# A constant tile 32 bytes longer: all tiles of matrix operands begin at a multiple of 128 bytes in each partition

## The chip, the cores and the metric

The kernel runs on one core of a Trainium2 chip. The metric is the device time of one execution in microseconds (us). Each partition of the on-chip memory (128 partitions) holds 224 KiB, and this kernel fills it almost to the last byte.

## What is computed

One layer with two parallel branches over a sequence of 256 rows of width 2048, all in float32:

```
h = rms_norm(x, norm_g);  proj = h @ w_in            # 2048 -> 11264 columns
q, k, v, z_a, u_b, v_b, z_b, g_a, g_b = split(proj)
att  = softmax(causal(rms_norm(q) rms_norm(k)^T / sqrt(128))) v     # 8 heads of 128
y_a  = (att * silu(z_a)) @ w_proj_a
sgu  = gelu(u_b) * (causal(w_spatial) @ rms_norm(gelu(v_b)) + b_spatial)
y_b  = (sgu * silu(z_b)) @ w_proj_b
out  = x + (sigmoid(g_a) * y_a + sigmoid(g_b) * y_b) @ w_out
```

## The kernel before, in words

**The stream of weights.** All weights pass through the core once, as 120 steps of 1 MB (128 partitions x 2048 words). `schedule` lists them in order: eight steps ("quad") each for q, k, v, za, vb, ub and zb, then four times eight steps of the gates g followed by four steps "proj" of the two branch projections, then sixteen steps of the output projection. SyncE's queue loads a step into one of six buffers `words`; ScalarE rounds it into a float32r tile `wh` (the high half), and VectorE writes the rest, the low half, back into the same buffer `words`, seen as float32r. `split` and `halve` (L228 to L266) do this, two or three steps ahead of the matmuls (the table `LEADS`).

**The matmuls.** Every product is made of three matmuls, recorded at one line, L416, in the helper `three`: low half of the activations with high half of the weights, high with high, high with low. The weights are the moving operand (512 columns), the activations the stationary operand (128 x 128). So of three matmuls in a row the first two stream a tile `wh` and the third streams `words`. 66 of the 120 steps are multiplied directly (24 matmuls; 16 of these are the "proj" steps), and 54 steps by a scheme with seven products in place of eight (21 matmuls); for the latter VectorE forms three sums of blocks into a buffer `sums` (L260 to L262), ScalarE rounds them into a tile `th` (L263), and VectorE takes the remainders in `words` (L265) and in `sums` (L266). That makes 2,718 matmuls of 512 columns. Between them stand transposes (L528, L588), the scores (L550), the attention's second product (L600, L602) and the spatial mixing (L616), all of 128 columns.

**The order on the engines** is written out by hand: `HOOKS` says behind which step each piece of the attention, the gating and the norms is issued, and all engines keep that order (`manual_schedule`).

**Where the tiles lie.** The six buffers `words` and three buffers `sums` are cut out of one block, `arena`, that starts in each partition at byte 1152, nine times 128, and all their sizes are multiples of 128. Behind it come the pools, in the order in which they are opened (L168 to L172): `const`, `big` (ten slots of 8192 bytes: the halves of the activations `xuh`, `xul`, `mh`, `ml`, `zah` and so on, the forms `Fhx`, `Flx`, the transposed `qT`, `kT`), `unit` (ten slots of 2048 bytes), `wpool` (four `wh` of 8192, three `th` of 6144) and `small`. A tile begins at the next multiple of 32 bytes. In `const` the order and the offsets are:

| tile | bytes | offset from a multiple of 128, before | after |
|---|---|---|---|
| vec | 104 | 0 | 0 |
| ident | 512 | 0 | 0 |
| mhalf | 32, then 64 | 0 | 0 |
| tri | 512 | 32 | 64 |
| gain | 512 | 32 | 64 |
| rstd | 8 | 32 | 64 |
| ssum | 8 | 64 | 96 |
| F5h, F5l | 2048 each | 96 | 0 |
| all of big, unit, wpool | 8192, 2048, 6144 | 96 | 0 |
| words and sums (arena) | 8192, 6144 | 0 | 0 |

So before, every stationary operand and the moving tiles `wh` and `th` begin 96 bytes past a multiple of 128, and the moving low halves (`words`, `sums`) at one. Slices of them that a matmul reads begin at multiples of 512 bytes from the start of the tile, so each matmul's operand has its tile's offset. The last tile of `small` ends 32 bytes below the end of the partition.

Of the kernel before, what the change touches and what calls it, by code (L numbers as in the profile page):

```python
# [14 lines left out]
F32 = mybir.dt.float32  # L15
# [7 lines left out]
P = 128  # L23
# [106 lines left out]
def hybrid_layer_kernel(  # L130
# [37 lines left out]
    const = ctx.enter_context(tc.tile_pool(name="const", bufs=1))  # L168
# [3 lines left out]
    small = ctx.enter_context(tc.tile_pool(name="small", bufs=4))  # L172
# [152 lines left out]

    ident = const.tile([P, P], F32, name="ident")
    make_identity(nc, ident)
    mhalf = const.tile([P, 8], F32, name="mhalf")
    nc.gpsimd.memset(mhalf[:, 0:4], -0.5)
    ninf = mhalf[:, 4:5]  # L330
    nc.gpsimd.memset(ninf, NEG_INF)
# [226 lines left out]
    def scores(hg, c):  # L558
        return X["S0", hg] if c == 0 else X["S1"][:, 4 * hg:4 * hg + 4, :]

    def soft_max(hg):
        for c in range(2):
            mx = small.tile([P, 4], F32, tag="mx", name="mx")
            nc.vector.reduce_max(mx, scores(hg, c), axis=AX.X)
            nm = X["nm", c, hg] = small.tile([P, 4], F32, tag="nm", name="nm")
            nc.vector.tensor_scalar_mul(nm, mx, -ATT_SCALE)
# [160 lines left out]
    def keep_vec():  # L727
        nc.scalar.copy(vec, vec0)

    fns = dict(load_nat=load_nat, keep_vec=keep_vec, forms_4=forms_4, forms_5=forms_5, forms=forms, stats=stats,  # L730
               halves_h=halves_h, halves_l=halves_l, halves_4=halves_4, squares=squares, root=root, norm=norm,
               turn_qk=turn_qk, score=score, soft_max=soft_max, soft_exp=soft_exp, soft_sum=soft_sum, turn_p=turn_p,
               func=func, attend=attend, load_mix=load_mix, turn_z=turn_z, causal_mix=causal_mix, mix=mix,
               spatial=spatial, gate_b=gate_b, turn_m=turn_m, forms_m4=forms_m4, halves_m4=halves_m4,
# [176 lines left out]
```

## Time and profile before

| | us |
|---|---|
| median of 3 runs | 670.65 (670.46 to 672.16) |
| the profiled execution | 671.46 |
| its span, from the first to the last instruction | 669.7 |
| PE (matmuls) busy | 663.1 (99%) |
| PEld (loads of the stationary operand, beside PE) busy | 539.4 (81%) |
| DVE (VectorE) busy | 598.0 (89%) |
| ACT (ScalarE) busy | 425.8 (64%) |
| POOL (GpSimd) busy | 59.1 (9%) |

Outside the span lie 1.8 us of the profiled execution. A matmul's recorded time runs from its start to the modelled end of its results, and the next one starts before that; the pace is read from start to start. In the rows below, "out<-moving,stationary" names a matmul's operands.

### The profile page before, as it was taken

The numbers are of one execution on the slowest core, as the hardware profiler recorded it, in microseconds if no ns is written. First come the engines' busy times: TensorE is split into PE (matmuls) and PEld (weight loads), VectorE is DVE, ScalarE is ACT, GpSimd is POOL, SyncE is SP. The second block draws the span as 40 slices with busy tenths as digits, with TensorE's granted clock in tenths as the row PEclk, the third lists the DMA queues.
The fourth block names the chain that finished last, engine by engine and source line by source line (L and its number), as shares of the span: only waits on it lengthen the run. The fifth ranks groups of instructions, "written<-read, shape, count | busy, mean of one in ns | idle before, by whom it ended". The sixth has DMA issues, their size and how long they took to land.

```text
span 669.7 us, 8157 instructions
## 1 busy us (share of the span) xinstructions
PE 663.1 (99%) x2974; PEld 539.4 (81%) x2974; DVE 598.0 (89%) x577; ACT 425.8 (64%) x534; POOL 59.1 (9%) x72
## 2 busy tenths in 40 slices
PE   8999999999999999999999999999999999999997
PEld 5888888888888888888888888888888888887885
DVE  4879998898978899899999899899989997899995
ACT  7968759957958567796465555654564556365450
POOL 1000203100000101200010001000100000000000
PEclk9999999999999999999999999999999999999999
DMA  8985686885677766786788579858975895786831
GB/s 299 419 319 186 242 237 224 266 238 187 220 227 208 258 201 223 260 224 248 211 292 253 188 243 276 293 188 260 294 235 197 273 291 182 246 259 222 247 126 63
DMA packets 42519, 159.46 MB, mean 238 GB/s; under 512 B 4720, under 2 KB 5360, under 8 KB 33264
## 3 DMA queue, kind: packets, MB, share of 16 engines
q1 hardware_dynamic: 34704, 144.80, 60.2%
q0 software_dynamic: 6624, 12.06, 12.3%
q10 hardware_dynamic: 1152, 2.10, 1.1%
q8 instruction: 23, 0.38, 0.2%
q14 instruction: 16, 0.13, 0.1%
HBM read 156.84 MB, written 26.21 MB: 273 GB/s over the span
## 4 chain that ended last, share of the span: by engine, by line
PE 98%; DMA 1%; ACT 0%; DVE 0%; SPq 0%; DVEq 0%; issue 0%
PE acc_g L416 15%; PE y L416 13%; PE acc_out L416 9%; PE seven_g L416 9%; PE acc_q L416 7%; PE acc_k L416 5%; PE acc_v L416 5%; PE acc_vb L416 5%; PE acc_zb L416 5%; PE acc_za L416 5%; PE acc_ub L416 5%; PE seven_out L416 3%; PE seven_k L416 2%; PE seven_zb L416 2%; PE seven_vb L416 2%; PE seven_za L416 2%
## 5 line engine op out<-in xcount | busy, mean ns | idle before, releaser
L214 POOL DMA_DIRECT2D ring<-in_w x46 | 38.3, 846 | 400.4 <-DMA ring<-in_w 400.4
L263 ACT CAST th<-sums1float 128x1536 fp32r<-128x1536 f32 x18 | 26.8, 1487 | 51.3 <-DVE sums1float L262 51.3
L263 ACT CAST th<-sums0float 128x1536 fp32r<-128x1536 f32 x18 | 26.6, 1479 | 44.1 <-DVE sums0float L262 44.1
L263 ACT CAST th<-sums2float 128x1536 fp32r<-128x1536 f32 x18 | 26.6, 1480 | 34.3 <-DVE sums2float L262 29.1
L416 PE MATMUL acc_g<-wh,xuh 128*128 128x512 f32 x105 | 41.3, 393 | 0.0
L416 PE MATMUL acc_g<-wh,xul 128*128 128x512 f32 x105 | 40.9, 390 | 0.0
L230 DVE TENSOR_TENSOR words5float32r<-words5float,wh 128x2048 fp32r<-128x2048 f32 x14 | 32.0, 2286 | 3.6 <-ACT wh L229 3.6
L266 DVE TENSOR_TENSOR sums1float32r<-sums1float,th 128x1536 fp32r<-128x1536 f32 x18 | 31.5, 1753 | 3.2 <-ACT th L263 3.2
L230 DVE TENSOR_TENSOR words4float32r<-words4float,wh 128x2048 fp32r<-128x2048 f32 x13 | 29.7, 2287 | 4.4 <-ACT wh L229 4.4
L266 DVE TENSOR_TENSOR sums2float32r<-sums2float,th 128x1536 fp32r<-128x1536 f32 x18 | 31.5, 1752 | 0.2 <-ACT th L263 0.2
L266 DVE TENSOR_TENSOR sums0float32r<-sums0float,th 128x1536 fp32r<-128x1536 f32 x18 | 31.6, 1753 | 0.0
L265 DVE TENSOR_TENSOR words2float32r<-words2float,wh 128x2048 fp32r<-128x2048 f32 x12 | 27.5, 2292 | 1.2
L416 PE MATMUL acc_out<-wh,mh 128*128 128x512 f32 x72 | 28.4, 394 | 0.0
L416 PE MATMUL acc_out<-wh,ml 128*128 128x512 f32 x72 | 28.3, 393 | 0.0
L416 PE MATMUL acc_q<-wh,xuh 128*128 128x512 f32 x64 | 26.3, 411 | 1.1 <-ACT wh L229 1.1
L229 ACT CAST wh<-words5float 128x2048 fp32r<-128x2048 f32 x14 | 26.6, 1904 | 0.1
L416 PE MATMUL acc_q<-wh,xul 128*128 128x512 f32 x64 | 25.9, 404 | 0.0
L229 ACT CAST wh<-words4float 128x2048 fp32r<-128x2048 f32 x13 | 24.9, 1916 | 1.5 <-PE y L416 0.9
L230 DVE TENSOR_TENSOR words1float32r<-words1float,wh 128x2048 fp32r<-128x2048 f32 x9 | 20.6, 2287 | 5.5 <-ACT wh L229 5.5
L416 PE MATMUL y<-wh,zal 128*128 128x512 f32 x64 | 25.2, 393 | 0.0
L416 PE MATMUL y<-wh,zah 128*128 128x512 f32 x64 | 25.2, 393 | 0.0
L416 PE MATMUL y<-wh,zbh 128*128 128x512 f32 x64 | 25.2, 393 | 0.0
(960 smaller groups left out, 2151.2 us busy)
## 6 DMA issues: line engine op xcount, KB each, us to landing
words4float<-in_w SPq DMA_DIRECT2D x15, 1024.0 KB, 6.5
words5float<-in_w SPq DMA_DIRECT2D x14, 1024.0 KB, 4.9
ring<-in_w SPq DMA_DIRECT2D x46, 256.0 KB, 6.6
ring<-in_w POOLq DMA_DIRECT2D x46, 256.0 KB, 6.9
words0float<-in_w SPq DMA_DIRECT2D x11, 1024.0 KB, 6.9
words1float<-in_w SPq DMA_DIRECT2D x11, 1024.0 KB, 8.3
words3float<-in_w SPq DMA_DIRECT2D x11, 1024.0 KB, 8.2
words2float<-in_w SPq DMA_DIRECT2D x11, 768.0 KB, 6.7
```

Source lines behind the costliest of these rows:

```text
L214: nc.gpsimd.dma_start(pre[i], w[i, :, B:2 * B], accum_op=ALU.add)
L229: nc.scalar.copy(h, r)
L230: nc.vector.tensor_tensor(l, r, f(h), op=ALU.subtract)
L263: nc.scalar.copy(th[i], t)
L265: nc.vector.tensor_tensor(wl[i], r, f(wh[i]), op=ALU.subtract)
L266: nc.vector.tensor_tensor(tl[i], t, f(th[i]), op=ALU.subtract)
L416: nc.tensor.matmul(acc, a, b, start=(start and n == 0), stop=(stop and n == 2))
```

## The change

The constant tile `mhalf` gets 16 words in place of 8, so 64 bytes in place of 32. Only words 0 to 4 of it are used, before and after. What is allocated behind it moves up by 32 bytes. To make room, the tile `mx` of the softmax (16 bytes, each in a place of 32) gets two buffers in place of the four that the pool gives by default, which frees 64 bytes at the end of the partition.

```diff
-    mhalf = const.tile([P, 8], F32, name="mhalf")
+    mhalf = const.tile([P, 16], F32, name="mhalf")
     nc.gpsimd.memset(mhalf[:, 0:4], -0.5)
     ninf = mhalf[:, 4:5]
...
-            mx = small.tile([P, 4], F32, tag="mx", name="mx")
+            mx = small.tile([P, 4], F32, tag="mx", bufs=2, name="mx")
             nc.vector.reduce_max(mx, scores(hg, c), axis=AX.X)
             nm = X["nm", c, hg] = small.tile([P, 4], F32, tag="nm", name="nm")
             nc.vector.tensor_scalar_mul(nm, mx, -ATT_SCALE)
```

## The prediction

> **What bounds the kernel now.** I read the profile's page first: who is busy, at which clock, and what the chain that ended last is made of.
>
> ```profile
> span 669.7 us, 8157 instructions
> ...
> PE 663.1 (99%) x2974; PEld 539.4 (81%) x2974; DVE 598.0 (89%) x577; ACT 425.8 (64%) x534; POOL 59.1 (9%) x72
> ...
> PEclk9999999999999999999999999999999999999999
> ...
> PE 98%; DMA 1%; ACT 0%; DVE 0%; SPq 0%; DVEq 0%; issue 0%
> ```
>
> TensorE is the chain: 98% of it, at the full granted clock. Since a busy PE is not PE at its peak, I asked next whether it ever waits (the waits of PE: microseconds in total, times, longest).
>
> ```profile
> PE ps_w L314 <- DVE warm L311: 1.3, 1, 1.3
> PE acc_q L416 <- ACT wh L229: 1.1, 1, 1.1
> ```
>
> That is all before a matmul; so the time is the number of matmuls times the interval from one start to the next. The chain in order of time gives that interval (start, us, line, count).
>
> ```profile
> 52.97 12.60 PE acc_k L416 x54
> ...
> 151.30 5.36 PE ps_s L550 x48
> ...
> 325.57 12.51 PE acc_g L416 x54
> ...
> 431.43 22.19 PE y L416 x96
> ```
>
> The reader is to divide. 12.60/54 is 233.3 ns, 12.51/54 is 231.7, 22.19/96 is 231.1. It is the same instruction each time (128x512, three per product), the same clock, no wait, and yet three paces. They are steady: I followed the intervals between starts through the whole timeline, and each stretch keeps its pace until a transpose or another 128-column instruction breaks the row; then it takes one of the three. Sorted so, 385 intervals run at 233.3 (up to 102 us), 1,149 at about 231.7 and 1,143 at 231.1 ns: 2,677 in all. The other 41 of the 2,718 matmuls stand in the slow start or beside a break.
>
> A pace that depends on how a row was entered, and then stays, is a rhythm that repeats. It repeats over three matmuls: 3 x 233.33 is 700.0 ns and 3 x 231.11 is 693.3; the middle one closes only after twelve, 12 x 231.67 = 2,780. All three are whole multiples of one step of 6.67 ns: 105, 104 and 417 of them. So something in the operand reads seems to be granted in turns of 6.67 ns, and what decides the turn differs between the three matmuls of a product. The groups by line, in the window of the fast rhythm and in that of the slow one, show which:
>
> ```profile
> L416 PE MATMUL y<-wh,zbh 128*128 128x512 f32 x16 | 6.3, 393 | 0.0
> L416 PE MATMUL y<-wh,zbl 128*128 128x512 f32 x16 | 6.2, 388 | 0.0
> ...
> L416 PE MATMUL y<-words0float32r,zbh 128*128 128x512 f32 x8 | 3.2, 398 | 0.0
> ```
>
> ```profile
> L416 PE MATMUL acc_q<-wh,xuh 128*128 128x512 f32 x24 | 9.5, 395 | 0.0
> L416 PE MATMUL acc_q<-wh,xul 128*128 128x512 f32 x24 | 9.4, 393 | 0.0
> L416 PE MATMUL acc_q<-words5float32r,xuh 128*128 128x512 f32 x8 | 3.2, 400 | 0.0
> ```
>
> A recorded time is the interval plus a tail that stays: the mean of 388, 393 and 398 is 393, less 231.1 leaves 162 ns. So in the fast rhythm the three take 226, 231 and 236 ns. The long one is each time the third, which streams `words`. It differs from the other two in its place in the order and in one more thing: `words` begins at a multiple of 128 bytes, `wh` and the stationary tiles 96 bytes past one. The shortest interval, 226 to 227 ns, is 34 steps of 6.67.
>
> **The change part by part.** *Offsets.* After the change `wh`, `th`, `words`, `sums` and all stationary tiles have the same offset, none. No instruction is added or removed; what changes is the interval. If the offset is what tells the three matmuls apart, they become alike, the rhythm closes after one matmul instead of three, and the interval itself must be a whole number of steps: 34 (226.67 ns) or 35 (233.33). The mean is now 34.7. I take 34, because two reads at one offset follow each other in 226 ns in the fast rhythm, and because what makes the third long there, the move from one offset to the other and back, is gone. Term by term: 385 x (233.33 - 226.67) = 2.6 us, 1,149 x (231.67 - 226.67) = 5.7 us, 1,143 x (231.11 - 226.67) = 5.1 us; together 13.4 us. The bounds of this term: 35 steps everywhere cost 1,149 x 1.67 + 1,143 x 2.22 = 4.5 us; one step below 34 (220 ns), for operands that no longer begin inside a turn, would save 2,677 x 11.67 = 31.2 us. Nothing in the trace is as short as 220.
>
> The Trainium skill (TensorE: Matmul & The Clock Gate, "Back-to-back issue gap") gives N/2.4 + 2.5 ns between isolated matmuls, 216 ns for 512 columns. By that figure, as an estimate, some 42 us would be there to be won; the trace's 231 does not agree with it, and no run here shows which part of the difference is the offset's.
>
> *Loads of the stationary operand.* They lie under the matmul before:
>
> ```profile
> L416 PEld LDWEIGHTS acc_g<-wh,xul 128*128 128x128 f32 x105 | 19.7, 188 | 4.6
> ```
>
> 188 ns against an interval of 227 leaves cover, so a shorter load saves nothing by itself.
>
> *Instructions of 128 columns.* The scores, whose operands lie at 96, take 5.36/48 = 111.7 ns each. Some 250 records are of that size; even two or three ns off each is under 0.8 us, in either direction, and I count it at nothing.
>
> *What a faster TensorE runs into.* VectorE prepares the weights:
>
> ```profile
> 300.00:400.00 100.00, 100.00 (x442) 81.34 (x441) 94.44 (x89) 59.76 (x45) 6.58 (x8) 1.00 0.75 235
> 400.00:500.00 100.00, 100.00 (x434) 81.11 (x434) 92.69 (x80) 55.41 (x40) 8.23 (x10) 1.00 0.83 261
> 500.00:600.00 100.00, 100.00 (x451) 81.61 (x450) 90.40 (x89) 54.90 (x48) 6.57 (x8) 1.00 0.76 241
> ```
>
> VectorE is busy 90 to 94 us of each 100 in the gates; TensorE would need 98. It fits as a total, and VectorE's work is one to thirteen us ahead of the first matmul that needs it. At one place it is not ahead, in the first output steps:
>
> ```profile
> 605.61 2.29 DVE L265 TENSOR_TENSOR words1float32r<-words1float,wh 128x2048 fp32r<-128x2048 f32 x1
> ...
> 607.68 0.40 PE L416 MATMUL acc_out<-wh,mh 128*128 128x512 f32 x1
> ...
> 607.96 0.19 PEld L416 LDWEIGHTS acc_out<-words1float32r,mh 128*128 128x128 f32 x1 [0.31 <-DVE words1float32r L265]
> ```
>
> The load waits for VectorE's subtraction and the matmul starts at 607.96 instead of 607.91. What TensorE wins in the row before it, 93 intervals x 4.44 ns = 0.4 us, is waited away there. The sum is 13.4 - 0.4 = 13.0 us.
>
> *The `mx` buffers and the tile itself.*
>
> ```profile
> L564 DVE TENSOR_REDUCE mx<-S x4: 678/946/1214, 161.3 to 170.2; 128x4 f32<-128x512 f32 x2, 128x4 f32<-128x1024 f32 x2
> L566 DVE TENSOR_SCALAR nm<-mx x4: 170/170/172, 162.0 to 171.5; 128x4 f32<-128x4 f32 x4
> ```
>
> Four maxima in all, each written and read by VectorE in its own order; the third goes into a buffer whose reader was two instructions earlier on the same engine. Nothing waits, nothing is queued behind it: zero. If a wait were put there all the same, it would be one of some 0.1 us, under the several us that the weights are ahead there. The fills of `mhalf` keep their size.
>
> The profiled execution is 671.46 us, 669.7 of span and 1.8 outside it; it lies 0.8 us above the median of the three runs. 671.46 - 13.0 = 658.5.
>
> **The rivals.** *No change (671.5).* The third matmul is long for its place in the order, not for its offset, and the paces stay. For it: the low half at a multiple of 128 is the slowest of the three now, so lying at one is no gain in itself. Against it: nothing else that I see would make two reads of the same row and a third of another row differ in so fixed a way. At most the rows fall into other rhythms: all at 231.11 would be 385 x 2.22 + 1,149 x 0.56 = 1.5 us less, which a measurement of this kernel cannot tell from none (it tells about 0.3%, 2.0 us). The Trainium skill (SBUF — State Buffer, "Operand start alignment") asks only for a start at a multiple of the element size, and the same page says under "Who interferes with whom" that "PE and ACT never wait on anyone". By that rule the change does nothing; the three paces of one instruction speak against it, but the rule has not been timed here.
>
> *Slower (675.9).* All operands now meet in the same turn, stationary and moving, and the one rhythm that is left is that of 35 steps: 233.33 ns everywhere, which is +4.5 us. It decides wherever a uniform row needs more than 34 steps. For it: the whole q and k part runs at that pace now, though with two offsets. Against it: the mean is below 35 steps with the offsets apart, and pairs at one offset are the shorter ones.
>
> *A smaller gain (667.0).* Only the third matmul changes and becomes like the other two:
>
> ```profile
> L416 PE MATMUL acc_g<-wh,xuh 128*128 128x512 f32 x105 | 41.3, 393 | 0.0
> L416 PE MATMUL acc_g<-wh,xul 128*128 128x512 f32 x105 | 40.9, 390 | 0.0
> ...
> L416 PE MATMUL acc_g<-words3float32r,xuh 128*128 128x512 f32 x44 | 17.4, 396 | 0.0
> ```
>
> 396.5 against a mean of 391.5 is 5 ns on every third matmul: 2,677 x 5 / 3 = 4.5 us.
>
> *A larger gain (about 650).* 220 ns, 31 us of TensorE; then TensorE would need 95 us where VectorE needs 94, and I take it that a third is given back to waits for VectorE, as at 607.96: some 21 us kept.
>
> **How the numbers follow.** Forecast (34 steps, 658.5) 0.39; smaller gain 0.16; larger gain 0.07; no change 0.23; slower 0.15. Faster by over 0.3% is the sum of the first three, 0.62; within 0.3% 0.23; slower 0.15. The range goes from 648, below the larger gain, to 673, above no change; it leaves out the slower case and a little below the larger gain. The forecast's own range is 655 to 661.
>
> **What would show it.** In the changed kernel the chain's long pieces should all give one interval, 12.2 us for 54 matmuls in k as in g and 21.8 for the 96 of a "proj" group, and the three groups of a product should have the same mean, about 389 ns. The wait on `words` near 607 us should grow to some 0.7 us. It is wrong if three paces remain (then the offset is not what sets them), if the one pace is 233 ns (then meeting in one turn costs), or if the interval is shorter but PE shows new waits for VectorE lines L230, L265 or L266 that add up to more than 2 us.

## The result, and the profile after

The changed kernel takes 659.45 us (median of 4 runs, 659.02 to 660.42) against 671.08 us of the kernel before (4 runs, 670.46 to 672.16): a ratio of 0.983, with an interval of 0.981 to 0.985. Its profiled execution took 659.17 us, 12.3 less than that of before; the forecast was 658.5.

The profile's page after, in the lines that answer to those of before:

```profile
span 657.4 us, 8157 instructions
...
PE 650.4 (99%) x2974; PEld 539.4 (82%) x2974; DVE 597.3 (91%) x577; ACT 425.6 (65%) x534; POOL 60.2 (9%) x72
...
PE 95%; DVE 2%; DMA 1%; issue 0%; ACT 0%; SPq 0%; DVEq 0%
```

The same instructions, the same work on every other engine; only TensorE's busy time has shrunk, by 12.7 us. The chain in order of time (start, us, line, count) gives the interval from matmul to matmul:

```profile
52.02 12.24 PE acc_k L416 x54
...
319.22 12.24 PE acc_g L416 x54
...
423.04 21.76 PE y L416 x96
```

12.24/54 and 21.76/96 are both 226.7 ns. The three paces of before (233.3, 231.7, 231.1) have become one. Of the 871 places where the three matmuls of one product are followed by another product, 850 take 680 ns from start to start, 3 x 226.67; nearly all others are the first ones after a break. The groups by line in a "proj" stretch show the three matmuls of a product alike:

```profile
L416 PE MATMUL y<-wh,zbl 128*128 128x512 f32 x16 | 6.2, 389 | 0.0
L416 PE MATMUL y<-wh,zbh 128*128 128x512 f32 x16 | 6.2, 389 | 0.0
...
L416 PE MATMUL y<-words0float32r,zbh 128*128 128x512 f32 x8 | 3.1, 389 | 0.0
```

389 less the tail of 162 is 227. Before, they stood at 388, 393 and 398.

What the faster stream runs into is seen in the waits of PE, where one row is new, and in the timeline at that place:

```profile
PE ps_w L314 <- DVE warm L311: 1.3, 1, 1.3
PE acc_q L416 <- ACT wh L229: 1.2, 1, 1.2
PE acc_out L416 <- DVE words1float32r L265: 0.3, 1, 0.3
```

```profile
596.15 0.39 PE L416 MATMUL acc_out<-wh,mh 128*128 128x512 f32 x1
...
596.83 0.19 PEld L416 LDWEIGHTS acc_out<-words1float32r,mh 128*128 128x128 f32 x1 [0.71 <-DVE words1float32r L265]
596.84 0.50 PE L416 MATMUL acc_out<-words1float32r,mh 128*128 128x512 f32 x1 [0.29 <-DVE words1float32r L265]
```

From 596.15 to 596.84 are 0.69 us instead of 0.23: 0.46 us lost, where the kernel before lost 0.05. The windows of the gates show how near VectorE has come to TensorE:

```profile
300.00:400.00 100.00, 100.00 (x451) 82.93 (x450) 97.10 (x90) 59.04 (x45) 7.39 (x9) 1.00 0.76 244
400.00:500.00 100.00, 100.00 (x443) 82.84 (x442) 94.67 (x83) 57.87 (x40) 7.42 (x9) 1.00 0.81 255
500.00:600.00 100.00, 99.71 (x456) 82.41 (x455) 92.10 (x89) 57.24 (x51) 6.58 (x8) 1.00 0.80 252
```

97.1 us of the busiest 100, where it was 94.4.

### The profile page after: what moved, and what is told of

Read it like the earlier page. It is cut to its first block, busy times and chain, and to the rows that moved or that the text cites. A ratio compares the mean times of both kernels' runs of the same rounds, so it can differ in the third digit from the quotient of the medians.

```text
span 657.4 us, 8157 instructions
## 1 busy us (share of the span) xinstructions
PE 650.4 (99%) x2974; PEld 539.4 (82%) x2974; DVE 597.3 (91%) x577; ACT 425.6 (65%) x534; POOL 60.2 (9%) x72
## 4 chain that ended last, share of the span: by engine, by line
PE 95%; DVE 2%; DMA 1%; issue 0%; ACT 0%; SPq 0%; DVEq 0%
PE acc_g L416 15%; PE y L416 13%; PE seven_g L416 9%; PE acc_out L416 7%; PE acc_q L416 7%; PE acc_vb L416 5%; PE acc_v L416 5%; PE acc_za L416 5%; PE acc_ub L416 5%; PE acc_zb L416 5%; PE acc_k L416 5%; PE seven_out L416 2%; PE seven_v L416 2%; PE seven_zb L416 2%; PE seven_ub L416 2%; PE seven_vb L416 2%
## 5 line engine op out<-in xcount | busy, mean ns | idle before, releaser
L416 PE MATMUL y<-wh,zbl 128*128 128x512 f32 x64 | 25.0, 390 | 0.0
```

The lines of the kernel that those rows point to most:

```text
L416: nc.tensor.matmul(acc, a, b, start=(start and n == 0), stop=(stop and n == 2))
```

## The experiments

The theory: what sets the interval is whether the operands have one offset. The rivals: that the start at a multiple of 128 itself is what is won; that only the moving operands' offsets, or only the stationary ones', count; that the buffers of `mx` did it. In what follows an offset is that of an operand's start from a multiple of 128 bytes. All layouts keep the instructions of the two kernels; only the lengths of small tiles and unused gaps differ, and line numbers move with them.

**The buffers alone.** The second line of the diff without the first.

```diff
-            mx = small.tile([P, 4], F32, tag="mx", name="mx")
+            mx = small.tile([P, 4], F32, tag="mx", bufs=2, name="mx")
```

> Only the second line of the change: mx with two buffers, mhalf as long as before, so that all operands lie as before. Both theories: no difference, 670.7 us within 0.3%, and the three paces of 233.3, 231.7 and 231.1 ns. A gain here would mean that the buffers, not the offsets, made it.

Measured: 670.78 us, ratio 1.000 (0.999 to 1.001). The buffers gave nothing. The paces are those of before, but the long row of matmuls that starts near 374 us changes its pace on the way:

```profile
493.78 22.19 PE y L416 x96
...
525.04 7.70 PE acc_g L416 x33
```

The first piece runs at 231.1 ns, the second at 233.3, where the kernel before kept 231.2 (7.63 us for the same 33). The change falls near 517.5 us, where no 128-column instruction stands and the waits of PE show nothing. The prediction had read from the kernel before that a pace lasts to the next break of the row; here it does not.

**One offset that is no multiple of 128.** The change, and a gap of 32 bytes ahead of the arena, so that every operand lies at 32.

```diff
+    nc.alloc_sbuf_tensor("gap", [P, 8], F32)
     nc.alloc_sbuf_tensor("arena", [P, (8 * RAWS + 6 * TS) * KB // 4], F32)
...
-    mhalf = const.tile([P, 8], F32, name="mhalf")
+    mhalf = const.tile([P, 16], F32, name="mhalf")
```

> All matrix operands, the low halves in words and sums among them, begin 32 bytes past a multiple of 128: one offset, but no multiple of 128. Theory (what costs is that the operands have different offsets): the changed kernel's one interval of 226.7 ns, some 659 us. Rival (the start at a multiple of 128 itself is what is won, a read that begins inside a turn pays one more step): 233.3 ns everywhere, about 676 us, or at least no less than the 671 of before.

Measured: 659.28 us, ratio 0.982 (0.981 to 0.984). Its chain in order of time:

```profile
320.06 12.24 PE acc_g L417 x54
423.86 21.76 PE y L417 x96
```

The same 226.7 ns as with the change. So a start at a multiple of 128 is worth nothing by itself; the gain is that all offsets agree.

**Moving operands at 0, stationary ones at 96.** `mhalf` as before and 32 unused bytes ahead of `wpool`, which holds `wh` and `th`.

```diff
+    padp = ctx.enter_context(tc.tile_pool(name="padp", bufs=1))
+    padp.tile([P, 8], F32, name="pad")
     wpool = ctx.enter_context(tc.tile_pool(name="wpool", bufs=6))
```

> All moving operands (wh, th, words, sums) begin at a multiple of 128, all stationary ones 96 bytes past one, as before. If the offsets of the three moving operands among each other are what costs: 226.7 ns, 659 us. If moving and stationary have to agree (the load of the next stationary operand and the stream beside it meet in a turn): another rhythm, 231 to 233 ns, 669 to 676 us. I expect the first, 60 to 40.

Measured: 675.33 us, ratio 1.006 (1.005 to 1.008), slower than before the change.

```profile
52.57 12.60 PE acc_k L418 x54
326.71 12.60 PE acc_g L418 x54
433.45 22.40 PE y L418 x96
```

12.60/54 and 22.40/96 are 233.3 ns, everywhere. The three moving operands agree here and the three matmuls of a product have the same mean; the pace is one, but of 35 steps of 6.67 ns and not of 34. The likelier of the two expectations fell: it does not suffice that the moving operands agree, stationary and moving must. The tiles of the weights, on which ScalarE and VectorE work beside the matmuls, have the same offset here as with the change, so it is not the offset of their accesses to the weights that makes the difference.

**High halves at 32, all else at 0.** The change, and the same 32 unused bytes ahead of `wpool`.

> The stationary operands and the low halves at a multiple of 128, the high halves wh and th 32 bytes past one. If the moving operands' offsets among each other are what costs: the three paces of before or paces like them, 231 to 233 ns, 669 to 676 us. If only the stationary operands' start matters: 226.7 ns and 659 us.

Measured: 670.46 us, ratio 0.999 (0.998 to 1.000).

```profile
52.71 12.60 PE acc_k L418 x54
325.43 12.48 PE acc_g L418 x54
431.18 22.19 PE y L418 x96
```

233.3, 231.1 and 231.1 ns: several paces again, as before the change, although all stationary operands and a third of the moving ones lie at 0. So the stationary operands' start alone does not decide either.

**64 bytes between the low halves and all else.** Two small tiles made one, which moves all behind them down by 32 bytes, from 96 to 64.

```diff
-    rstd = const.tile([P, 2], F32, name="rstd")
-    ssum = const.tile([P, 2], F32, name="ssum")
+    both_sums = const.tile([P, 4], F32, name="both_sums")
+    rstd, ssum = both_sums[:, 0:2], both_sums[:, 2:4]
```

> The low halves at a multiple of 128, everything else 64 bytes past one; two small tiles are made one for that, mx keeps its four buffers. If offsets count by 128 bytes: paces of 231 to 233 ns, 669 to 676 us. If they count by 64 bytes: 226.7 ns, 659 us. I expect 64 bytes, 55 to 45, since the step of 6.67 ns at 226.7 ns for 2,048 bytes is the time of some 60 bytes.

Measured: 672.12 us, ratio 1.002 (1.001 to 1.003). 12.53 us for the 54 matmuls in k and in g, 232.0 ns. Offsets do not count by 64 bytes: the likelier of the two expectations fell.

**Stationary operands at 64, and at 32, all moving ones at 0.** The layout of the 96-byte run with other lengths; for the second, `nm` is computed in the place of `mx` and one small pool has seven buffers in place of eight, to make room.

```diff
+    padp.tile([P, 16], F32, name="pad")      # first: 64, with the two small tiles made one
...
+    padp.tile([P, 24], F32, name="pad")      # second: 32, with mhalf of 24 words
```

> All moving operands at a multiple of 128, all stationary ones 64 bytes past one. Theory (a stream and the load of a stationary operand beside it share reads in turns, and pass each other without loss only at the same offset): not below 226.7 ns; 233.3 as with 96 bytes, 675 us, or another value between. Rival (offsets count by 64 bytes): 226.7 ns, 659 us. After the run with 64 bytes between the halves, at 232.0 ns, I give the rival 0.15.

> All moving operands at a multiple of 128, all stationary ones 32 bytes past one (the other side of the 96 bytes measured). If any difference between the two kinds costs one step: 233.3 ns, 675 us. If the sign of the difference counts (the load ahead of the stream or behind it): another interval, possibly one below 226.7 ns and under 659 us; I give that 0.2.

Measured: with 64, 664.42 us, ratio 0.991 (0.989 to 0.992); with 32, 675.45 us, ratio 1.007 (1.005 to 1.009). Their chains, the 64 first:

```profile
52.28 12.36 PE acc_k L418 x54
321.74 12.36 PE acc_g L418 x54
426.51 21.97 PE y L418 x96
```

```profile
52.89 12.60 PE acc_k L418 x54
327.01 12.60 PE acc_g L418 x54
433.75 22.40 PE y L418 x96
```

So with all moving operands alike, a difference to the stationary ones of 0, 32, 64 and 96 bytes gives 226.7, 233.3, 228.9 and 233.3 ns. The sign does not matter (32 and 96 are alike), half of 128 costs a third of what these cost, and no difference that was tried goes below 226.7. With 64 bytes the three matmuls of a product are not alike, although all three have the same two offsets (440 to 446 us):

```profile
L418 PE MATMUL y<-wh,zbh 128*128 128x512 f32 x10 | 3.9, 388 | 0.0
L418 PE MATMUL y<-wh,zbl 128*128 128x512 f32 x9 | 3.5, 394 | 0.0
L418 PE MATMUL y<-words0float32r,zbh 128*128 128x512 f32 x5 | 2.0, 392 | 0.0
```

Less the tail of 162 these are some 226, 232 and 230 ns.

**Short loads.** Is it the load of a stationary operand that meets the stream? Three kernels cut loads to a quarter, by using 32 of the 128 stationary columns, which leaves out three quarters of what these matmuls compute: in the second matmul of each product, then in nearly all matmuls, with the operands at one offset and with the stationary ones at 96.

```diff
+            if n == 1 and not first:                                  # one load in three
+                nc.tensor.matmul(acc[0:32, :], a[:, 0:32], b, start=False, stop=False)
+                continue
...
+            if not (start and n == 0) and not (stop and n == 2):      # nearly all loads
+                nc.tensor.matmul(acc[0:32, :], a[:, 0:32], b, start=False, stop=False)
+                continue
             nc.tensor.matmul(acc, a, b, start=(start and n == 0), stop=(stop and n == 2))
```

> The changed kernel, but the second of the three matmuls of each product (high half with high half) uses only 32 of its 128 stationary columns, so that three quarters of the main products are left out; its load is a quarter as long, its stream of 512 columns stays. Theory (part of the interval is paid for a load that runs beside the stream): of the three intervals the one beside which the short load runs, from the first matmul's start to the second's, falls below 226.7 ns, to some 218; the two others stay. Rival (the interval is the stream's own and the loads beside it cost nothing): all three stay at 226.7 ns.

> The changed kernel, but of nearly all matmuls (all that neither open nor close a sum) only 32 of the 128 stationary columns are used, which leaves out three quarters of the products. All loads are short (108 ns in place of 188) and alike again; the streams of 512 columns stay. If the mix of long and short loads was what broke the rhythm of the run with one short load in three: 226.7 ns again. If the length of a load costs: less, 216 to 220 ns. If neither: 231 to 233 ns, as in that run.

> The same short loads in the layout with all moving operands at a multiple of 128 and all stationary ones 96 bytes past one, which took 233.3 ns with full loads. If stationary and moving reads disturb each other while a load runs, a load of a quarter of the columns disturbs less: below 233.3, 226 to 229 ns. If the offset alone fixes the interval, whatever the length of the load: 233.3 ns.

Measured, by one profile each: spans of 668.2, 667.9 and 669.1 us, and mean intervals of 231.1, 231.3 and 231.5 ns, single ones mostly from 225 to 238. The loads did become short; the groups of one load in three, and of nearly all:

```profile
L419 PEld LDWEIGHTS acc_g<-wh,xul 128*128 128x128 f32 x105 | 19.7, 188 | 4.7
...
L417 PEld LDWEIGHTS acc_g<-wh,xuh 128*32 128x32 f32 x105 | 11.3, 108 | 4.6
```

```profile
L417 PEld LDWEIGHTS acc_g<-wh,xuh 128*32 128x32 f32 x105 | 11.5, 109 | 12.1
```

With one short load in three neither expectation held. With nearly all loads short the third one held, 231 to 233 ns; in the layout with 96 bytes the mean lies between the two expected values. Shorter loads did not make the stream faster, and making nearly all of them short did not bring 226.7 back, so the mixing of lengths was not what broke the rhythm. A matmul that uses 32 columns also writes 32 rows of its sum in place of 128, so these kernels change more than the load, and what a shorter load alone would do is not shown.

The two layouts with short loads have nearly the same mean, but not the same paces. At one offset, then with the stationary operands at 96:

```profile
67.09 7.65 PE acc_k L417 x33
302.26 7.64 PE acc_zb L417 x33
```

```profile
68.05 7.48 PE acc_k L419 x33
302.79 7.70 PE acc_zb L419 x33
```

The first two are 231.8 and 231.5 ns, the others 226.7 and 233.3. So the offset still matters with short loads, and the nearness of the means is no sign that it does not. Whether the load is what meets the stream, these runs do not show.

## Why the prediction was right, point by point

*The bound.* TensorE was the bound, and all of the gain is in its interval: 2,677 intervals of a mean of 231.67 ns before, 2,675 of 226.82 after.

*The term of the sum.* 34 steps, 226.67 ns, was forecast and is what the rows of the chain show. The term was 13.4 us; the means give 2,677 x 4.85 = 13.0. The missing 0.4 is the first few intervals after each break, which still take 231 to 236 ns until the rhythm has settled.

*What it runs into.* Near 596 us 0.4 us were to be waited away, with a load's wait grown from 0.31 to some 0.7: the row shows 0.71, and 0.41 us more lost than before. A tenth of a microsecond more is lost at 508 us, in the third group of gates, which I did not foresee: a load waits there for VectorE's product `g_h`.

```profile
507.86 0.19 PEld L416 LDWEIGHTS seven_g<-wh,Flx 128*128 128x128 f32 x1 [0.25 <-DVE g_h L685]
```

13.0 - 0.4 - 0.1 is 12.5; the span shows 12.3.

*The `mx` buffers.* Counted at zero; alone they gave 1.000.

*The reason.* It held in part. The offsets do set the rhythm: the rival "no change" is refuted by the result, and "a start at a multiple of 128" by the run with all operands at 32. But the step that chose between 34 and 35 stood on the wrong pair. I argued that three matmuls which become alike leave only 34 or 35, and took 34 because two *moving* reads at one offset follow each other in 226 ns. With the moving reads all alike and the stationary ones 96 bytes away the three have the same offsets just as well, and the interval is 35 steps. With the stationary ones 64 bytes away they have the same offsets too, and yet take some 226, 232 and 230 ns, 228.9 on average, which is neither 34 steps nor 35. So matmuls with the same offsets need not become alike, nor need the interval be a whole number of steps. What 34 needs, in the runs here, is that stationary and all moving operands agree.

The rows of before could not have told this. Both `wh` matmuls of a product had their two operands at 96, and yet took 226 and 231 ns. Nor does it go matmul by matmul: in the run with 64 bytes between the low halves and all else, two matmuls of three have operands that agree. By the 226.7 and 228.9 ns of the runs with all moving operands alike, the mean would be 227.4 ns; it was 232.0. The rival that I called "slower" had this the wrong way round as well: it said that meeting in one turn costs a step, and it is not meeting that does. So the sum was right because the change happens to align all operands at once, and that was luck as far as this step goes; a change that had aligned the weights alone would have been forecast at 658.5 and measured at 675.3.

*What the pages said.* The Trainium skill (SBUF — State Buffer, "Who interferes with whom") gives TensorE two read ports, one for the stream and one for the loads, and lets it wait on no other engine. The Trainium skill (TensorE: Matmul & The Clock Gate, "Step-by-step: what each phase is for") adds that loading the next stationary operand takes no read bandwidth from the running matmul. For these float32r matmuls the runs sit badly with the second: with all moving operands at one offset, where the stationary operand lies moves the interval between 226.7 and 233.3 ns. That it does so through its load is argued, not shown.

*What stays open.* Why the agreement of offsets saves a step; whether it is a matmul's own stationary operand or the next one, loaded beside it, that has to agree; why short loads give 231.3 ns at one offset; and whether 128 bytes is the period at all. In the changed kernel the constant tiles ahead of `F5h` take 1,792 bytes, so that `words` and the tiles behind them lie a multiple of 256 bytes apart, and no run sets all operands to agree modulo 128 but not modulo 256. No run here separates these.

## What to carry to other kernels

Where a stream of identical matmuls runs without waits but at more than one pace, compare the byte offsets of the operands before looking for work to remove: here 32 bytes of padding were worth 1.7%, without an instruction more or less. Give stationary and moving operands the same offset (modulo 128 bytes, or 256 to be as in these runs). Aligning the moving ones alone cost 0.6 to 0.7% where the stationary ones lay 32 or 96 bytes off, and gained 0.9% where they lay 64 off. And test such a rule at an offset that is not zero, since only that tells "aligned" from "alike".

## What the runs showed that I had not expected

- A difference of 32 bytes between stationary and moving operands costs as much as one of 96 (233.3 ns), one of 64 much less (228.9 ns against 226.7 with none). But 64 bytes between the low halves and all else gave 232.0 ns.
- A load of 32 columns takes 108 ns where one of 128 takes 188, so most of the short one is not per column; and with matmuls of 32 columns, whose loads these are, the mean interval at one offset was 231.3 ns against 226.8.
- With the operand offsets of before, the same row of matmuls held 231.1 ns to its end in one run and went over to 233.3 ns near 517.5 us in another, without a break in the row and without a wait in the list.
